# Four of seven Strassen-Winograd products added up in one PSUM bank, with their partial sums copied out by ScalarE

## The chip, the cores and the metric

The kernel runs on one core of a Trainium2 chip. In the profile the engines are PE (TensorE's matmuls) and PEld (its weight loads), DVE (VectorE), ACT (ScalarE), POOL (GpSimd) and SP (SyncE, which here only issues DMAs). The metric is device microseconds for one execution of the whole program; lower is better.

## The reference, cut to what matters

The program is one layer of a decoder trunk in float32, for 256 tokens of width 2048: a mixer with differential attention, a convolution and retention, then cross-attention, then a gated feed-forward net of hidden width 5632. What fills the time are its dense products:

```
proj = h @ w_in                      # 2048 x 14336
merged = sum over 3 branches of sigmoid(gates) * (y @ w_branch[i])
x = x + merged @ w_out
q = h @ wq ; k, v = split(m @ wkv) ; x = x + o @ wo
a, b = split(h @ w13) ; x = x + (silu(a) * b) @ w2
```

## The kernel before

**One product.** A float32 operand is split in two fp32r parts, hi (a rounded copy, made by an ACT cast into a tile `wh`) and lo (what is left, made by a DVE subtraction into `wl`). One 128 x 512 result then takes three matmuls for each 128 rows of weight: hi*hi, hi*lo and lo*hi (`products`). Weights come in chunks `raw` of 128 x 2 x 512 (512 KB) by DMAs from SP; there are ten `raw` buffers and five each of `wh` and `wl`. A **unit** is one chunk with its matmuls: 12 where it serves both halves of the tokens ("N"), 6 where it serves one ("S"). `emit_unit` makes the parts of up to four units ahead of the one that is multiplied, so the casts run until they wait for PE to give back a `wh` buffer.

**A pair.** `pair` computes two neighbouring blocks of 512 output columns, W0 and W1, for all 256 tokens. The 2048 rows of weight are four chunks of 512. With `MODES2` two of them go through Strassen-Winograd: seven products p1 to p7 in place of eight, on sums of weight blocks (made by DVE and by accumulating DMAs from POOL) and sums of activation blocks (made by `factors`). The other two chunks are plain N units. `MODES1` has one S chunk and three N chunks. There are 26 pairs: five for the gates, four for keys and values, two for `w_out`, one for `w_o`, ten for the feed-forward columns (numbers 1 to 10 here) and four for `w_2`. Between some of them lie plain blocks (`block`), and small side tasks (transposes, softmax, normalisation) are mixed in.

**PSUM.** Eight banks of 512 columns: two tiles `mm` of two banks (one column block for both token halves) and four tiles `tp` of one bank, shared with the side tasks. In a pair, `ps0` and `ps1` are `mm` tiles, `pp` holds `tp` tiles. p2 and p4 go to `ps0` and p3 to `ps1`, with the N units. p1, p5, p6 and p7 each get a `tp` bank (summed over the S chunks) and are combined outside PSUM: `join1` copies p1 to SBUF on ACT, `join5`, `join6` and `join7` are five DVE operations of 512 columns, and `done` adds what they left to `ps0` and to `ps1` with one DVE operation of 1024 columns each, before the block's `evac`.

**Order.** The tile framework places the instructions of each engine when the program is built and adds the semaphore waits. Engines run their own lists in order. A wait on a PSUM tile counts for the whole tile: a matmul into one bank of an `mm` tile waits for a copy out of the other bank too.

Of the kernel before, what the change touches and what calls it, by code (L numbers as in the profile page):

```python
# [13 lines left out]
ALU = mybir.AluOpType  # L14
# [43 lines left out]
def trunk(ctx, tc, xT, xtok, memT, memtok, w_in, w_br, w_out, w_q, w_kv, w_o, w_13, w_2,  # L58
          prm, cst, decay, gfin, out):
    nc = tc.nc  # L60
    P = 128
# [231 lines left out]
    def products(u, only=None, final=True):  # L293
        a = u["act"]
        for k in range(2):
            for ps, key, k0, t, kind in u["prods"]:
                if only is not None and t not in only:
                    continue
                ah, al = lhs(a, kind, (t, k0) if kind == "n" else t, k)
                o = ps[key]  # L300
                fl = (id(ps), key)
                pe.matmul(o, ah, u["hi"][:, k, :], start=fl in u["start"] and k == 0, stop=False)
                pe.matmul(o, ah, u["lo"][:, k, :], start=False, stop=False)
                pe.matmul(o, al, u["hi"][:, k, :], start=False, stop=fl in u["stop"] and k == 1)

    def emit_unit(i):
        while state["made"] < min(i + 1 + min(LA, 1 + i), len(units)):
# [24 lines left out]
    def quad_jobs(pp, ps0, ps1, w0, w1, a):  # L332
# [49 lines left out]
        def f3(u):  # L382
            r = raw(ix["b22"])
            add(t["a"], r)
            parts(u, r)
            raws.pop(ix["b22"])
# [18 lines left out]
    def pair(W0, W1, acts, modes, evac0, evac1):  # L405


        ps0, ps1, pp = {}, {}, {}
        xs = []
        us = []  # L410
        sset = [c for c in range(len(acts)) if modes[c] == "S"]
        nset = [c for c in range(len(acts)) if modes[c] == "N"]

        def enter():
            settle(3)
            cap[0] = 3
            pin[0] = True

        def join1():
            x0, x1 = S4([P, 2, 512]), S4([P, 2, 512])  # L420
            xs.extend([x0, x1])
            sc.copy(x0[:, 0, :], pp.pop(1))

        def join5():
            ve.tensor_tensor(out=xs[1][:, 1, :], in0=pp.pop(5), in1=xs[0][:, 0, :], op=ALU.add)

        def join6():

            p = pp.pop(6)
            ve.tensor_tensor(out=xs[1][:, 0, :], in0=p, in1=xs[1][:, 1, :], op=ALU.subtract)  # L430
            ve.tensor_tensor(out=xs[0][:, 1, :], in0=p, in1=xs[0][:, 0, :], op=ALU.subtract)

        def join7():
            p = pp.pop(7)
            ve.tensor_tensor(out=xs[0][:, 1, :], in0=p, in1=xs[0][:, 1, :], op=ALU.subtract)
            ve.tensor_tensor(out=xs[1][:, 1, :], in0=xs[1][:, 0, :], in1=p, op=ALU.subtract)
            cap[0] = 4

        def done(n, ps, evac):
            def f():  # L440
                x = xs[n]
                ve.tensor_tensor(out=x, in0=ps["m"], in1=x, op=ALU.add)
                xs[n] = None
                insb[0] = True
                evac(x)
                insb[0] = False
# [6 lines left out]
        def units_of(*names):  # L453
            return [q[n] for m in names for q in quads for n in m]

        first = units_of(("p1",), ("p2", "p5"), ("p3", "p6"))
        marks = {len(quads) - 1: join1, 3 * len(quads) - 1: join5, 5 * len(quads) - 1: join6}

        def marked(i, f):
            def g():  # L460
                u = f()
                if i in marks:
                    call(marks[i])
                return u
            return g

        us += mixed([marked(i, f) for i, f in enumerate(first)], n0)
        us += [f() for f in units_of(("p7",))]
        call(join7)
        us += mixed(units_of(("p4",)), n1[:len(n1) // 2])  # L470
        call(done(0, ps0, evac0))
        us += [f() for f in n1[len(n1) // 2:]]
        call(done(1, ps1, evac1))

        def unpin():
            pin[0] = False

        call(unpin)
        close(us)

    def pair_n(W0, W1, acts, evac0, evac1, after):
# [114 lines left out]
    def factors(a, q):  # L596
# [4 lines left out]
        for o, x, y, op in ((0, a22, a21, ALU.subtract), (2, a11, a21, ALU.subtract),  # L601
                            (1, a22, fv[:, 2], ALU.add), (3, a12, fv[:, 1], ALU.subtract)):
# [977 lines left out]
```

## Time and profile before

| | |
|---|---|
| three runs | 2001.64, 2002.55, 1997.3 us; median 2001.64 |
| the profiled execution | 1998.88 us, span 1997.1 us |
| PE, PEld | 1979.9 us (99%), 1636.8 us (82%), 9081 of each |
| DVE | 1666.9 us (83%) |
| ACT | 1120.4 us (56%) |
| TensorE's granted clock | 0.999 of full speed |

The pairs lie between about 500 and 1905 us of the span. Matmuls overlap in the profile: the record of one runs on while the next has started, so a busy PE is judged by the distance from one start to the next and by the idle time listed ahead of an instruction.

### The profile page before, as it was taken

The numbers are of one execution on the slowest core, as the hardware profiler recorded it, in microseconds if no ns is written. First come the engines' busy times: TensorE is split into PE (matmuls) and PEld (weight loads), VectorE is DVE, ScalarE is ACT, GpSimd is POOL, SyncE is SP. The second block draws the span as 40 slices with busy tenths as digits, with TensorE's granted clock in tenths as the row PEclk, the third lists the DMA queues.
The fourth block names the chain that finished last, engine by engine and source line by source line (L and its number), as shares of the span: only waits on it lengthen the run. The fifth ranks groups of instructions, "written<-read, shape, count | busy, mean of one in ns | idle before, by whom it ended". The sixth has DMA issues, their size and how long they took to land.

```text
span 1997.1 us, 25285 instructions
## 1 busy us (share of the span) xinstructions
PE 1979.9 (99%) x9081; PEld 1636.8 (82%) x9081; DVE 1666.9 (83%) x2040; ACT 1120.4 (56%) x1343; POOL 129.8 (6%) x172
## 2 busy tenths in 40 slices
PE   9999999999999999999999999999999999999998
PEld 7888888888788887888888888888888878878886
DVE  6997689778887788989988565899988999889974
ACT  7444343548655556655566554665655665655653
POOL 0000000000100001000111000000001000011000
PEclk9999999999999999999999999999999999999999
DMA  9656555554777788689898544957888978988891
GB/s 377 206 193 197 180 177 166 180 170 151 214 208 240 235 262 257 221 263 283 274 295 304 191 158 136 287 177 224 271 274 276 275 231 252 301 278 260 256 329 61
DMA packets 128285, 463.88 MB, mean 232 GB/s; under 512 B 14368, under 2 KB 14624, under 8 KB 128160
## 3 DMA queue, kind: packets, MB, share of 16 engines
q1 hardware_dynamic: 105552, 380.46, 54.1%
q0 software_dynamic: 22464, 81.80, 19.3%
q8 instruction: 71, 1.16, 0.2%
q14 instruction: 54, 0.44, 0.1%
q10 hardware_dynamic: 144, 0.01, 0.0%
HBM read 449.63 MB, written 12.58 MB: 231 GB/s over the span
## 4 chain that ended last, share of the span: by engine, by line
PE 79%; issue 9%; DVE 6%; DMA 4%; POOL 1%; ACT 1%; SPq 0%; ACTq 0%; POOLq 0%; DVEq 0%
PE mm L86 64%; PE tp L86 15%; DVE wl L86 3%; DVE s L86 2%; DMA raw<-in_w 2%; DMA raw<-in_w_kv 1%; DMA raw<-in_w_in 1%; POOL raw L94 1%; DVE raw L86 1%; ACT wh L86 1%; DMA s<-in_memtok 0%; SPq L97 0%; POOL s L94 0%; ACTq L1575 0%; POOL x2d L94 0%
## 5 line engine op out<-in xcount | busy, mean ns | idle before, releaser
L86 PE MATMUL mm<-wh,s 128*128 128x512 f32 x4568 | 1443.9, 391 | 3.5 <-ACT wh L86 3.3
L86 ACT CAST wh<-raw 128x1024 fp32r<-128x1024 f32 (+1 forms) x855 | 886.4, 1051 | 728.7 <-PE mm L86 474.9
L86 DVE TENSOR_TENSOR wl<-raw,wh 128x1024 fp32r<-128x1024 f32 (+1 forms) x855 | 1020.8, 1217 | 252.7 <-ACT wh L86 241.3
L86 PEld LDWEIGHTS mm<-wh,s 128*128 128x128 f32 x4568 | 857.7, 188 | 183.1 <-ACT wh L86 7.0
L86 PE MATMUL mm<-wl,s 128*128 128x512 f32 x2284 | 893.2, 391 | 4.4 <-DVE wl L86 4.4
L86 PEld LDWEIGHTS mm<-wl,s 128*128 128x128 f32 x2284 | 429.5, 188 | 97.3 <-DVE wl L86 9.3
L86 PE MATMUL tp<-wh,s 128*128 128x512 f32 x864 | 288.5, 392 | 0.0
L86 PEld LDWEIGHTS tp<-wh,s 128*128 128x128 f32 x864 | 162.2, 188 | 33.1
L86 PE MATMUL tp<-wl,s 128*128 128x512 f32 x432 | 168.1, 389 | 0.0
L86 DVE TENSOR_TENSOR s<-s,s 128x1024 f32<-128x1024 f32 (+4 forms) x144 | 140.8, 986 | 1.7 <-ACT wh L86 1.1
L86 DVE TENSOR_TENSOR s<-tp,s 128x512 f32<-128x512 f32 (+1 forms) x166 | 109.6, 683 | 16.4 <-PE tp L86 11.7
L86 DVE TENSOR_TENSOR raw<-raw,raw 128x1024 f32<-128x1024 f32 x100 | 121.0, 1216 | 0.4
L86 DVE SCALAR_TENSOR_TENSOR s<-s,prm_t,s 128x256 fp32r<-128x256 f32 (+25 forms) x256 | 105.8, 461 | 0.0
L86 DVE TENSOR_TENSOR s<-mm,s 128x1024 f32<-128x1024 f32 (+1 forms) x70 | 83.1, 1187 | 20.3 <-PE mm L86 20.1
L86 PEld LDWEIGHTS tp<-wl,s 128*128 128x128 f32 x432 | 81.2, 188 | 16.2
L86 ACT ACTIVATE s<-s 128x512 f32<-128x512 f32 (+1 forms) x60 | 46.2, 771 | 63.3 <-DVE s L86 51.4
L94 POOL DMA_DIRECT2D raw<-in_w x54 | 47.7, 883 | 431.8 <-DVE wl L86 188.4
L86 PE MATMUL tp<-cst_t,s 128*128 128x128 f32 x408 | 57.1, 272 | 0.0
L86 PEld LDWEIGHTS tp<-cst_t,s 128*128 128x128 f32 x408 | 48.6, 140 | 9.0 <-issue 0.3
L86 PE MATMUL tp<-s,s 128*128 128x256 f32 (+4 forms) x348 | 53.5, 314 | 0.0
L86 PEld LDWEIGHTS tp<-s,s 128*128 128x128 f32 (+1 forms) x348 | 46.1, 189 | 5.8 <-issue 0.5
L86 ACT COPY s<-tp 128x512 f32<-128x512 f32 (+1 forms) x69 | 35.8, 528 | 15.0 <-PE tp L86 13.3
(88 smaller groups left out, 503.2 us busy)
## 6 DMA issues: line engine op xcount, KB each, us to landing
raw<-in_w SPq DMA_DIRECT2D x264, 512.0 KB, 6.5
raw<-in_w_in SPq DMA_DIRECT2D x239, 512.0 KB, 4.6
raw<-in_w_kv SPq DMA_DIRECT2D x64, 512.0 KB, 5.4
raw<-in_w POOLq DMA_DIRECT2D x54, 512.0 KB, 8.5
raw<-in_w_br SPq DMA_DIRECT2D x48, 512.0 KB, 6.5
raw<-in_w_out SPq DMA_DIRECT2D x32, 512.0 KB, 7.6
raw<-in_w_q SPq DMA_DIRECT2D x32, 512.0 KB, 5.1
raw<-in_w_o SPq DMA_DIRECT2D x32, 512.0 KB, 4.0
```

The costliest lines, as they stand in the source:

```text
L86: i = f(*a, **k)
L94: tc.keep_in_program_order(nc.gpsimd.dma_start(**kw))
```

## The change

The roles of the two blocks change, and four products are added up by TensorE. p1, p6, p7 and p4 now go, in this order, to one bank of `ps1` (key 1), p2 to its other bank (key 0), and p3 to `ps0`; only p5 still has a `tp` bank, which it holds until after p7. ACT copies the state of the shared bank to SBUF after p1 (`keep1`), after p6 and after p7 (`keep`), and its end in `done1`. DVE subtracts the copies from p5 (`keep`, 512 columns twice), adds `ps0` (1024 columns) and one bank of `ps1` (512 columns). p6 moves ahead of p3 and takes the load of the block b22 with it; the last N unit of `ps0` moves behind p7, and `done0` with its `evac` ahead of p4. `factors` has other signs and as many operations.

```
-        return dict(p1=unit(pp, 1, 0, 0, "n", f1, b11=w0[:, 0:2, :]),
-                    p2=unit(ps0, 0, 2, 0, "n", f2, b21=b21, b12=w1[:, 0:2, :]), p5=unit(pp, 5, 0, 0, "s", f5),
-                    p3=unit(ps1, 0, 0, 3, "s", f3, b22=b22), p6=unit(pp, 6, 0, 1, "s", f6),
-                    p7=unit(pp, 7, 0, 2, "s", f7), p4=unit(ps0, 1, 2, 1, "n", f4))
+        return dict(p1=unit(c1, 1, 0, 0, "n", f1, b11=w0[:, 0:2, :]),
+                    p2=unit(c1, 0, 2, 0, "n", f2, b21=b21, b12=w1[:, 0:2, :]), p5=unit(pp, 5, 0, 0, "s", f5),
+                    p6=unit(c1, 1, 0, 1, "s", f6, b22=b22), p3=unit(c2, 0, 0, 3, "s", f3),
+                    p7=unit(c1, 1, 0, 2, "s", f7), p4=unit(c1, 1, 2, 1, "n", f4))
...
+        def keep1():
+            xs.extend([S4([P, 2, 512]), S4([P, 2, 512])])
+            sc.copy(xs[1][:, 0, :], ps1[1])
+
+        def keep(i):
+
             def f():
+                x = xs[0][:, i, :]
+                sc.copy(x, ps1[1])
+                ve.tensor_tensor(out=x, in0=pp[5], in1=x, op=ALU.subtract)
+                if i:
+                    pp.pop(5)
+                    cap[0] = 4
             return f
 
+        def done0():
+            x = xs[0]
+            ve.tensor_tensor(out=x, in0=ps0["m"], in1=x, op=ALU.add)
...
+        def done1():
+            x = xs[1]
+            ve.tensor_tensor(out=x[:, 0, :], in0=ps1[0], in1=x[:, 0, :], op=ALU.add)
+            sc.copy(x[:, 1, :], ps1[1])
...
-        quads = [quad_jobs(pp, ps0, ps1, W0[c], W1[c], acts[c]) for c in sset]
+        quads = [quad_jobs(pp, ps1, ps0, W1[c], W0[c], acts[c]) for c in sset]
...
+        us += mixed(units_of(("p1",), then=keep1) + units_of(("p2", "p5"))
+                    + units_of(("p6",), then=keep(0)) + units_of(("p3",)), n0[:-1])
+        us += [f() for f in units_of(("p7",), then=keep(1))]
+        us.append(n0[-1]())
+        call(done0)
         us += mixed(units_of(("p4",)), n1[:len(n1) // 2])
```

**First place: p7 and p4 in feed-forward pair 2, on PE.** Before, `tp_2335` is p7's bank, `mm_2297` is `ps0` and `mm_2319` is `ps1`; wh_2326 is p7's second unit, wh_2328 is p4's first:

```order
L86 MATMUL tp_2335_11878<-wh_2326_11834,s4_2190_11208 128x512
L86 MATMUL mm_2297_11695<-wh_2328_11844,s4_2163_11075 128x512
L86 MATMUL tp_2335_11878<-wl_2327_11835,s4_2190_11208 128x512
L86 MATMUL tp_2335_11878<-wh_2326_11834,s4_2191_11209 128x512
L86 MATMUL tp_2335_11878<-wh_2326_11834,s4_2190_11208 128x512
L86 MATMUL tp_2335_11878<-wl_2327_11835,s4_2190_11208 128x512
L86 MATMUL tp_2335_11878<-wh_2326_11834,s4_2191_11209 128x512
L86 MATMUL mm_2319_11798<-wh_2331_11858,s4_2207_11294 128x512
```

Now `mm_2245` is `ps1`, wh_2282 is p7's second unit and wh_2287 is p4's first, all in one bank:

```order
L86 MATMUL mm_2245_11615<-wl_2283_11777,s4_2154_11172 128x512
L86 MATMUL mm_2245_11615<-wh_2282_11776,s4_2155_11173 128x512
L86 MATMUL mm_2245_11615<-wh_2282_11776,s4_2154_11172 128x512
L86 MATMUL mm_2245_11615<-wl_2283_11777,s4_2154_11172 128x512
L86 MATMUL mm_2245_11615<-wh_2282_11776,s4_2155_11173 128x512
L86 MATMUL mm_2245_11615<-wh_2287_11798,s4_2127_11039 128x512
L86 MATMUL mm_2245_11615<-wl_2288_11799,s4_2127_11039 128x512
L86 MATMUL mm_2245_11615<-wh_2287_11798,s4_2128_11040 128x512
```

p4 began in a bank of its own while p7 still ran; now it follows p7 in the same bank with nothing between, and its first matmul waits for the copy that ACT makes of that bank after p7's last. So it stands in pairs 1, 2, 5 and 6 of the feed-forward net; in the first pair of the gates two 128 x 128 transposes lie between; in the other 21 pairs there are 11 to 13 matmuls there.

**Second place: from feed-forward pair 9 to pair 10, on ACT.** Before, the end of the pair has no operation on ACT; `s4_3088` is pair 9's first result, and the casts wh_3145 on are of its last units and of the next pair's first:

```order
L86 ACTIVATE s4_3088_15441<-s4_3088_15441 128x1024
L86 CAST wh_3145_15711<-raw_3143_15705 128x1024
L86 CAST wh_3148_15729<-raw_3147_15727 128x1024
L86 CAST wh_3150_15747<-raw_3137_15673 128x1024
L86 CAST wh_3158_15771<-raw_3156_15765 128x1024
L86 CAST wh_3163_15788<-raw_3162_15786 128x1024
L86 CAST wh_3167_15804<-raw_3140_15685 128x1024
L86 CAST wh_3170_15825<-raw_3169_15822 128x1024
```

Now `mm_3008` is pair 9's `ps1`, and the copy is that of `done1`:

```order
L86 CAST wh_3072_15651<-raw_3062_15599 128x1024
L86 CAST wh_3075_15672<-raw_3074_15670 128x1024
L86 CAST wh_3083_15696<-raw_3081_15690 128x1024
L86 COPY s4_3017_15370<-mm_3008_15337 128x512
L86 CAST wh_3087_15711<-raw_3065_15611 128x1024
L86 CAST wh_3091_15729<-raw_3062_15599 128x1024
L86 CAST s4_3078_15683<-tp_3080_15685 128x512
```

One copy has been put between the casts of the next pair's units. The cast ahead of it (wh_3083) waits until PE has given back the `wh` of pair 10's p1; the copy waits for `done1`'s addition on DVE as well. PE's list has p1 of pair 10 (12 matmuls, in the tile that `ps0` left), and then the first N unit into the tile that this copy empties: from the matmul that frees wh_3083's buffer to that N unit there are six matmuls. It is so at ten ends of a pair: that of the first `w_out` pair and nine among the feed-forward and `w_2` pairs; at the others there are more matmuls or a plain block.

**Third place: p6 and p7 in feed-forward pair 1 (`MODES1`), on ACT.** Before, there are casts alone between the parts of p6, p7 and p4; s4_2239 is a part of an activation factor, made by `factors`:

```order
L86 CAST wh_2247_11458<-raw_2193_11215 128x1024
L86 CAST wh_2251_11473<-raw_2250_11471 128x1024
L86 CAST wh_2254_11491<-raw_2253_11489 128x1024
L86 CAST wh_2257_11509<-raw_2256_11507 128x1024
L86 CAST s4_2239_11425<-s4_2235_11401 128x1024
L86 CAST wh_2261_11524<-raw_2260_11522 128x1024
L86 CAST wh_2264_11536<-raw_2263_11534 128x1024
L86 CAST wh_2267_11554<-raw_2266_11552 128x1024
```

Now `mm_2175` is `ps1`, and the last row stands for the copies after p6 and after p7:

```order
L86 CAST wh_2210_11422<-raw_2157_11179 128x1024
L86 CAST wh_2213_11434<-raw_2212_11432 128x1024
L86 CAST wh_2216_11452<-raw_2215_11450 128x1024
L86 CAST wh_2219_11466<-raw_2218_11464 128x1024
L86 CAST s4_2203_11388<-s4_2199_11365 128x1024
L86 COPY s4_2180_11285<-mm_2175_11268 128x512 x2
```

The copy after p6 has moved behind wh_2219 and s4_2203. wh_2219 waits for the last matmul ahead of p7 on PE (its `wh` buffer), and p7's first matmul waits for the copy; p4 then follows p7 directly and waits for the second copy.

## Rows read from the trace of the kernel before

**Rows 1.** Page, part 1: engine, busy us (share of span) xinstructions.
```profile
span 1997.1 us, 25285 instructions
PE 1979.9 (99%) x9081; PEld 1636.8 (82%) x9081; DVE 1666.9 (83%) x2040; ACT 1120.4 (56%) x1343; POOL 129.8 (6%) x172
```

**Rows 2.** Busy time of each engine by stretch.
```profile
core 0: us, PE busy (x) PEld busy (x) DVE busy (x) ACT busy (x) POOL busy (x), PEclk, DMA share, GB/s
500.00:1905.00 1405.00, 1397.54 (x6380) 1157.80 (x6379) 1204.87 (x1248) 819.55 (x934) 120.65 (x158) 1.00 0.80 246
...
700.00:1100.00 400.00, 397.74 (x1785) 327.75 (x1784) 355.81 (x372) 241.12 (x288) 40.00 (x55) 1.00 0.86 271
...
1300.00:1900.00 600.00, 596.00 (x2662) 491.86 (x2661) 547.53 (x540) 354.79 (x366) 54.86 (x69) 1.00 0.84 256
...
```

**Rows 3.** Waits of the span: engine and line, releaser, us, times, longest.
```profile
PEld mm L86 <- DVE wl L86: 9.3, 13, 1.4
...
PEld mm L86 <- ACT wh L86: 7.0, 8, 1.6
...
PE mm L86 <- DVE wl L86: 4.4, 7, 1.0
...
PE mm L86 <- ACT wh L86: 3.3, 5, 1.2
```

**Rows 4.** Timeline 1545.6 to 1549.6 us: start, us, engine, line, operation [idle before <-releaser].
```profile
1546.13 0.61 PE L86 MATMUL tp<-wh,s 128*128 128x512 f32 x2
...
1546.82 0.61 PE L86 MATMUL tp<-wh,s 128*128 128x512 f32 x2
...
1547.49 0.39 PE L86 MATMUL tp<-wh,s 128*128 128x512 f32 x1
...
1547.72 0.39 PE L86 MATMUL mm<-wh,s 128*128 128x512 f32 x1
...
1547.92 0.59 ACT L86 COPY s<-tp 128x512 f32<-128x512 f32 x1 [0.26 <-PE tp L86]
...
1548.40 2.00 ACT L86 CAST wh<-raw 128x1024 fp32r<-128x1024 f32 x2
```

**Rows 5.** Timeline 1700 to 1702 us.
```profile
1700.45 0.39 PE L86 MATMUL mm<-wh,s 128*128 128x512 f32 x1
1700.62 1.99 ACT L86 CAST wh<-raw 128x1024 fp32r<-128x1024 f32 x2 [5.23 <-DMA raw<-in_w]
...
1701.72 0.50 PE L86 MATMUL mm<-wh,s 128*128 128x512 f32 x1 [0.88 <-ACT wh L86]
```

**Rows 6.** Groups of ACT, shapes apart: count | busy us, mean ns | idle before.
```profile
L86 ACT CAST wh<-raw 128x1024 fp32r<-128x1024 f32 x853 | 885.2, 1052 | 727.2 <-PE mm L86 474.9 <-DMA raw<-in_w 63.0 <-PE tp L86 39.5
...
L86 ACT COPY s<-tp 128x512 f32<-128x512 f32 x50 | 28.8, 589 | 6.0 <-PE tp L86 4.3 <-DVE s L86 1.7
L86 ACT CAST s<-s 128x1024 fp32r<-128x1024 f32 x24 | 25.2, 1049 | 10.1 <-DVE s L86 10.0
```

**Rows 7.** Groups of DVE, shapes apart, same columns.
```profile
L86 DVE TENSOR_TENSOR wl<-raw,wh 128x1024 fp32r<-128x1024 f32 x853 | 1019.4, 1218 | 251.1 <-ACT wh L86 239.7 <-DMA raw<-in_w_in 5.1 <-DMA raw<-in_w_q 4.5
...
L86 DVE TENSOR_TENSOR s<-mm,s 128x1024 f32<-128x1024 f32 x66 | 80.3, 1217 | 5.2 <-PE mm L86 5.0
L86 DVE TENSOR_TENSOR s<-tp,s 128x512 f32<-128x512 f32 x108 | 71.7, 683 | 11.8 <-PE tp L86 11.7
...
L86 DVE TENSOR_TENSOR s<-s,tp 128x512 f32<-128x512 f32 x26 | 17.6, 676 | 0.0
```

**Rows 8.** Timeline of ACT near 1375 us, and at 1575 us.
```profile
1375.51 1.06 ACT L86 CAST wh<-raw 128x1024 fp32r<-128x1024 f32 x1 [1.89 <-PE mm L86]
...
1575.18 3.90 ACT L86 CAST wh<-raw 128x1024 fp32r<-128x1024 f32 x4
```

More of the change, by code (lines that the diff above doesn't have):

```diff
@@ L301, in products @@
                 fl = (id(ps), key)
-                pe.matmul(o, ah, u["hi"][:, k, :], start=fl in u["start"] and k == 0, stop=False)
-                pe.matmul(o, ah, u["lo"][:, k, :], start=False, stop=False)
-                pe.matmul(o, al, u["hi"][:, k, :], start=False, stop=fl in u["stop"] and k == 1)
+                sk = dict(skip_group_check=True) if ps.get("open") and key == 1 else {}
+                pe.matmul(o, ah, u["hi"][:, k, :], start=fl in u["start"] and k == 0, stop=False, **sk)
+                pe.matmul(o, ah, u["lo"][:, k, :], start=False, stop=False, **sk)
+                pe.matmul(o, al, u["hi"][:, k, :], start=False, stop=(fl in u["stop"] or "ends" in u) and k == 1, **sk)
     def emit_unit(i):
@@ L330, in block, with quad_jobs @@
         call(lambda: evac(ps["m"]))
-    def quad_jobs(pp, ps0, ps1, w0, w1, a):
+    def quad_jobs(pp, c1, c2, w0, w1, a):
         def unit(ps, key, k0, t, kind, fn, **w):
@@ L380, in f5, with f3 @@
             parts(u, t["a"])
[L382 to L386, printed above, removed]
         def f6(u):
+            t["r"] = raw(ix["b22"])
+            add(t["a"], t["r"])
             parts(u, t["a"])
             gd(out=t["a"], in_=b21, accum_op=ALU.add)
+        def f3(u):
+            parts(u, t.pop("r"))
+            raws.pop(ix["b22"])
         def f7(u):
@@ L396, in f4 @@
             parts(u, t.pop("a"))
-        return dict(p1=unit(pp, 1, 0, 0, "n", f1, b11=w0[:, 0:2, :]),
-                    p2=unit(ps0, 0, 2, 0, "n", f2, b21=b21, b12=w1[:, 0:2, :]), p5=unit(pp, 5, 0, 0, "s", f5),
-                    p3=unit(ps1, 0, 0, 3, "s", f3, b22=b22), p6=unit(pp, 6, 0, 1, "s", f6),
-                    p7=unit(pp, 7, 0, 2, "s", f7), p4=unit(ps0, 1, 2, 1, "n", f4))
+        return dict(p1=unit(c1, 1, 0, 0, "n", f1, b11=w0[:, 0:2, :]),
+                    p2=unit(c1, 0, 2, 0, "n", f2, b21=b21, b12=w1[:, 0:2, :]), p5=unit(pp, 5, 0, 0, "s", f5),
+                    p6=unit(c1, 1, 0, 1, "s", f6, b22=b22), p3=unit(c2, 0, 0, 3, "s", f3),
+                    p7=unit(c1, 1, 0, 2, "s", f7), p4=unit(c1, 1, 2, 1, "n", f4))
     insb = [False]
     def pair(W0, W1, acts, modes, evac0, evac1):
-        ps0, ps1, pp = {}, {}, {}
+        ps0, ps1, pp = {}, {"open": True}, {}
         xs = []
@@ L416, in enter @@
             cap[0] = 3
[L417 to L439, printed above, removed]
-            def f():
[L441 to L446, printed above, removed]
-            return f
+        def keep1():
+            xs.extend([S4([P, 2, 512]), S4([P, 2, 512])])
+            sc.copy(xs[1][:, 0, :], ps1[1])
@@ new lines, in keep @@
+        def keep(i):
+            def f():
+                x = xs[0][:, i, :]
[4 more added lines that the diff above has]
+                    cap[0] = 4
+            return f
+        def done0():
+            x = xs[0]
+            ve.tensor_tensor(out=x, in0=ps0["m"], in1=x, op=ALU.add)
+            xs[0] = None
+            insb[0] = True
+            evac0(x)
+            insb[0] = False
@@ L449, in pair @@
+        def done1():
+            x = xs[1]
+            ve.tensor_tensor(out=x[:, 0, :], in0=ps1[0], in1=x[:, 0, :], op=ALU.add)
+            sc.copy(x[:, 1, :], ps1[1])
+            xs[1] = None
+            insb[0] = True
+            evac1(x)
+            insb[0] = False
         call(enter)
-        quads = [quad_jobs(pp, ps0, ps1, W0[c], W1[c], acts[c]) for c in sset]
+        quads = [quad_jobs(pp, ps1, ps0, W1[c], W0[c], acts[c]) for c in sset]
         n0, n1 = (each_half(ps, [W[c] for c in nset], [acts[c] for c in nset]) for ps, W in ((ps0, W0), (ps1, W1)))
-        def units_of(*names):
-            return [q[n] for m in names for q in quads for n in m]
@@ L456, in pair, with units_of, last @@
[L456 to L463, printed above, removed]
-                return u
[L465 to L469, printed above, removed]
+        def units_of(*names, then=None):
+            fs = [q[n] for m in names for q in quads for n in m]
+            def last():
+                u = fs[-1]()
+                u["ends"] = True
+                call(then)
+                return u
+            return fs if then is None else fs[:-1] + [last]
@@ L470, in pair @@
+        us += mixed(units_of(("p1",), then=keep1) + units_of(("p2", "p5"))
[3 more added lines that the diff above has]
+        call(done0)
         us += mixed(units_of(("p4",)), n1[:len(n1) // 2])
-        call(done(0, ps0, evac0))
         us += [f() for f in n1[len(n1) // 2:]]
-        call(done(1, ps1, evac1))
-        def unpin():
-            pin[0] = False
@@ L478, in pair @@
-        call(unpin)
+        call(done1)
         close(us)
@@ L600, in factors @@
         a11, a12, a21, a22 = (q[:, 2 * k:2 * k + 2, t * P:(t + 1) * P] for t in range(2) for k in range(2))
-        for o, x, y, op in ((0, a22, a21, ALU.subtract), (2, a11, a21, ALU.subtract),
-                            (1, a22, fv[:, 2], ALU.add), (3, a12, fv[:, 1], ALU.subtract)):
+        for o, x, y, op in ((0, a21, a22, ALU.subtract), (2, a11, a21, ALU.subtract),
+                            (1, fv[:, 0], a11, ALU.subtract), (3, a12, fv[:, 1], ALU.add)):
             ve.tensor_tensor(out=fv[:, o], in0=x, in1=y, op=op)
```

## The prediction

> **What bounds the kernel now.** I read the page's table of engines first, then the busy time by stretch, the waits, and a few microseconds of timeline. PE is busy for 1979.9 of the span's 1997.1 us [rows 1]. A busy PE may still run slower than it could, so I looked at starts: with 128x512 matmuls following each other, the one at 1546.13 and the one at 1547.49 are six apart, 1.36/6 = 0.227 us each, and where nothing is listed as idle it keeps that step [rows 4]. What is left for any other engine to spoil is small: between 500 and 1905 us, where all 26 pairs lie, PE is idle for 1405.00 - 1397.54 = 7.5 us [rows 2]. The waits that PE names there are for `wl` and `wh`, 4.4 and 3.3 us in the whole span, and for its weight loads 9.3 and 7.0 us, which overlap [rows 3]. One such place is at 1701.72: a cast waited 5.23 us for its weights, and PE lost 0.88 us [rows 5]. So PE is the bound, DVE is close behind (355.8 of 400 us from 700, 547.5 of 600 us from 1300), and ACT has room (354.8 of 600) [rows 2]. The casts spend 474.9 us waiting for PE to hand back a buffer [rows 6]: the stages behind PE run ahead of it as far as their buffers let them.
>
> **What the change removes.** The number of matmuls, their shapes and their weight loads stay as they are, and so does the step of 0.227 us: PE's own work is worth 0. DVE loses three operations in each pair. Before: four of 0.683 and one of 0.676 us (the latter group has 26 members, one for each pair) and two of 1.217; after: three of 0.683 and one of 1.217 [rows 7]. That is 5.84 - 3.27 = 2.57 us a pair, 26 x 2.57 = 67 us of DVE. In the stretch from 1300, which holds 14 of the pairs, DVE falls from 547.5 by 36 to about 512 of 600 us. None of it stands on PE's path except where PE waited for a late `wl`. The bounds of this gain are 0 and the whole 7.5 us; part of those 7.5 is late weights, as at 1701.72, which a freer DVE helps only through buffers that come back sooner. I take 3 us.
>
> **What it adds on ACT.** One PSUM copy a pair becomes four. The one of before took 589 ns [rows 6], so it is 3 x 0.589 x 26 = 46 us; from 1300 on, ACT rises by 14 x 1.77 = 25 to 380 of 600 us. As sheer work that is hidden behind PE. What counts is that PE now waits for these copies: after p6 and after p7 the next product goes to the bank that ACT is reading.
>
> The price of one such wait comes from the copy of p1 in the kernel before. The last p1 matmul starts at 1547.49, and its record ends 0.39 later, at 1547.88; the copy starts at 1547.92 and ends at 1548.51 [rows 4]. PE starts 0.05 us after ACT has ended: the cast of 1700.62 takes 1.05, and PE goes on at 1701.72 [rows 5, 6]. From the last matmul's start to the next into the same bank that is 0.39 + 0.04 + 0.59 + 0.05 = 1.07 us, where PE alone would take 0.23: **0.84 us** if nothing stands between. With eleven matmuls between, 12 x 0.227 = 2.72 us have gone by, and the wait is covered with 1.65 us to spare, even behind one more cast of 1.05.
>
> Place by place, from the order of the changed kernel:
> - p7 to p4 back to back, in feed-forward pairs 1, 2, 5 and 6: 4 x 0.84 = 3.4 us. In the first gate pair two small transposes stand between; I count 0.6. The other 21 pairs have 11 to 13 matmuls there and count 0, covered by the last N unit.
> - p6 to p7 in feed-forward pair 1. PE's last matmul frees a buffer; ACT casts wh_2219 (0.95 us to the next start in a row of casts, (3.90 - 1.05)/3 [rows 8]), casts an activation factor (0.95; 1.049 alone [rows 6]), and then copies: 0.39 + 0.04 + 0.95 + 0.95 + 0.59 + 0.05 - 0.23 = 2.7 us.
> - The ten ends of a pair where ACT has cast, copy, and PE six matmuls until it wants the tile: 0.39 + 0.04 + 0.95 + 0.59 + 0.05 = 2.02 against 7 x 0.227 = 1.59: 0.43 us each, 4.3 together. That the cast ahead of the copy does wait for PE, so that no slack is left in it, is what the 1.89 us at 1375.51 show of its kind [rows 8]; if it runs early, this item is 0.
> - p1 to p2: p2 lies in the same tile and waits for the copy of p1. There are at least six matmuls between in every pair (1.36 us more than the step, against 0.84), and three places where short ACT operations stand ahead of the copy: 0 to 1 us each. I take 1 us in all.
>
> The sum is 3.4 + 0.6 + 2.7 + 4.3 + 1 = 12.0 us.
>
> **What moves.** b22's load on SP and its addition come with p6 instead of p3, one or two units earlier, and its `raw` buffer of ten is held until p3's parts are made: SP's later loads may come a unit later, and the casts waited for weights for 63.0 us even before [rows 6]. Against that, DVE returns buffers sooner. POOL's second accumulating DMA, issued after that addition, comes earlier too, and p4 wants it later. I take 0 for these, between -2 and +6 us: a late weight has cost 0.88 us once [rows 5], and six more of it would be 6. p5's bank is held longer, but p1, p6 and p7 give theirs back to the side tasks. The signs in `factors` cost nothing: as many operations in as long a chain. `done0` comes earlier, which takes its 1.217 us out of the crowd around p4 [rows 7].
>
> **The sum.** -3 + 12.0 + 0 = +9 us on the profiled execution's 1998.88: 2007.9. That execution lies 2.8 us below the median of the three runs, 2001.64, so a median could come out up to 2.8 higher; I forecast **2009 us**. With the items at their ends the forecast's own range is 2005 to 2016.
>
> **The rivals.**
>
> *No change to be told (31%).* A stall of PE gives SP, ACT and DVE time to catch up. The new waits could then take the place of the 7.5 us that PE was idle anyway, and the ten ends of pairs could cost nothing if their casts run early: 3.4 + 0.6 + 2.7 + 1 - 5 = +3 us, 2002 to 2005 as above. For it speaks that the old idle time lies in the same stretches; against it, that the back-to-back places stand in the order whatever else happens.
>
> *Faster (5%).* If all of the 7.5 us goes back to DVE's lag, and the copies start while PE is held up by something else, the kernel ends at 1998.9 - 7.5 = 1991. The point from which it decides is 0: the new waits have to be below what DVE gives back. A stronger form is that DVE sets the pace wherever it is 89 to 91% busy, so that its 67 us come off whole: 1998.9 - 67 = 1932. The trace speaks against it: matmuls follow each other at a steady 0.227 us with DVE at that share, and PE's idle time bounds the gain at 7.5 us [rows 2, 4]; I give it 1 of the 5%. The Trainium skill (Perfetto Trace Analysis, Identifying the Most-Contended Engine) would lean to that form: it ranks engines by occupancy, but has TensorE judged by the occupancy of its weight loads since matmul records overlap, and PEld's 82% lies below DVE's share. Here the trace disagrees, as the even step of the matmuls shows.
>
> *Much slower (12%).* The copy after p7 blocks ACT's list. In 21 pairs it is covered by 11 to 13 matmuls, 1.65 us to spare, but if the cast ahead of it waits for weights, as casts did 22 times for one source alone [rows 6], the copy is late as well and PE stops with work at hand. At 0.84 us for each of 21 pairs it adds 18 us: 2007.9 + 18 = 2026. It decides from about 1.65 us of lateness. Against it: with the same weights late, PE would often have had to wait in the kernel before.
>
> **How the numbers follow.** Forecast 52%, no change 31%, much slower 12%, faster 5%. A measurement of this kernel can tell about 0.3% from no change, 6 us; nearly all of the forecast's case lies past that, and I count it as slower. So slower 0.64, same 0.31, faster 0.05. The range from 1999 to 2022 takes in the forecast's own, most of the case of no change and a half of the much slower one.
>
> **What would show it.** In the changed profile DVE's total falls by some 67 us and ACT's rises by 46; the copies out of `mm` are 104, near 0.59 us each. PE's idle time from 500 to 1905 us rises from 7.5 to about 16, and waits of PE on an ACT copy appear: 0.84 us at p4 in feed-forward pairs 1, 2, 5, 6, one of about 2.7 us in pair 1, and about 0.4 us at ends of pairs. Wrong would be: no wait of PE behind a copy; PE's idle time below 7.5 us; a step of matmuls other than 0.227 us; or new idle time that names `wl` or late weights instead.

## The result

The changed kernel takes 2016.87 us (median of six runs, 2014.67 to 2022.03) where the kernel before takes 2000.73 (six runs): a ratio of 1.0085, 95% interval 1.0070 to 1.0101, which is 14 to 20 us. The forecast was slower by 7 to 9 us; it is slower by 16. The profiled execution is the slowest of the six, 2022.03 us; what follows explains that one first and then what is usual.

Page, part 1, of the changed kernel:

```profile
span 2020.3 us, 25231 instructions
PE 1990.8 (99%) x9081; PEld 1640.3 (81%) x9081; DVE 1624.5 (80%) x1962; ACT 1161.7 (58%) x1421; POOL 129.8 (6%) x172
```

The same 9081 matmuls [rows 1]; DVE is busy for 42 us less, ACT for 41 us more, and the program is longer. Busy time by stretch, all the pairs first, then three short stretches (columns as in [rows 2]):

```profile
500.00:1905.00 1405.00, 1388.05 (x6287) 1145.22 (x6286) 1146.86 (x1156) 845.88 (x996) 114.89 (x150) 0.99 0.79 243
793.00:800.00 7.00, 6.72 (x19) 5.48 (x20) 6.45 (x9) 5.31 (x7) 2.87 (x5) 0.54 0.70 242
1374.00:1380.00 6.00, 5.50 (x14) 4.40 (x15) 4.27 (x4) 3.40 (x4) 0.00 (x0) 0.53 0.32 104
1805.00:1811.00 6.00, 5.84 (x19) 4.67 (x20) 6.00 (x7) 3.05 (x4) 0.00 (x0) 0.72 0.95 358
```

PE is idle for 17.0 us (1405.00 - 1388.05) where it was 7.5 [rows 2]. Look also at the third column from the end: in the three short stretches the mean granted clock is 0.54, 0.53 and 0.72 of full speed, between the levels of 1.2 and 2.4 GHz (0.50 and 1.00) and in two of them close to the lower. In the kernel before it was 1.00 in every stretch shown [rows 2]. What PE waits for (columns as in [rows 3]):

```profile
PEld mm L86 <- ACT s L86: 23.6, 23, 3.2
...
PE mm L86 <- ACT s L86: 13.8, 19, 2.7
...
PEld mm L86 <- DVE wl L86: 5.3, 8, 1.4
...
PE mm L86 <- DVE wl L86: 2.7, 5, 1.1
PE mm L86 <- ACT wh L86: 2.0, 4, 1.2
```

The old waits for `wl` and `wh` shrank from 4.4 and 3.3 us to 2.7 and 2.0 [rows 3]; the 13.8 us behind ACT's `s`, which are its copies of the shared bank, are new. The copies themselves, and the DVE operations that answer to [rows 6, 7]:

```profile
L86 ACT COPY s<-mm 128x512 f32<-128x512 f32 x104 | 60.5, 586 | 20.4 <-PE mm L86 19.9 <-DVE s L86 0.3
L86 DVE TENSOR_TENSOR s<-mm,s 128x1024 f32<-128x1024 f32 x40 | 48.7, 1219 | 2.9 <-PE mm L86 2.8
L86 DVE TENSOR_TENSOR s<-tp,s 128x512 f32<-128x512 f32 x56 | 38.3, 685 | 5.9 <-PE tp L86 4.2 <-ACT s L86 1.6
...
L86 DVE TENSOR_TENSOR s<-mm,s 128x512 f32<-128x512 f32 x30 | 20.6, 686 | 18.0 <-PE mm L86 18.0
```

**The three predicted waits** are where they were put. Feed-forward pair 2, p7's last matmul, the copy, p4's first (timeline of PE and ACT):

```profile
1423.20 0.39 PE L86 MATMUL mm<-wh,s 128*128 128x512 f32 x1
1423.63 0.59 ACT L86 COPY s<-mm 128x512 f32<-128x512 f32 x1 [0.30 <-PE mm L86]
...
1424.27 0.50 PE L86 MATMUL mm<-wh,s 128*128 128x512 f32 x1 [0.68 <-ACT s L86]
...
1424.61 0.39 PE L86 MATMUL mm<-wl,s 128*128 128x512 f32 x1
```

From start to start 1.07 us, so 0.84 lost, the price that the prediction made from [rows 4, 5]. (The bracket shows less, 0.68, since the record of the last matmul runs on.) The last row shows a part of the price that nobody had: behind the wait one more step takes 0.34 us (1424.61 - 1424.27) and not 0.227. It is so behind nearly every wait of both kernels, 0.11 us each time, and makes the whole price of such a wait 0.95. The end of pair 2 has the cast, the copy behind it, and the matmul that wants the tile:

```profile
1439.61 1.05 ACT L86 CAST wh<-raw 128x1024 fp32r<-128x1024 f32 x1 [0.30 <-PE mm L86]
...
1440.50 0.39 PE L86 MATMUL mm<-wh,s 128*128 128x512 f32 x1
1440.57 0.57 ACT L86 COPY s<-mm 128x512 f32<-128x512 f32 x1
...
1441.19 0.50 PE L86 MATMUL mm<-wh,s 128*128 128x512 f32 x1 [0.31 <-ACT s L86]
```

0.69 from start to start where 0.23 is the step: 0.46 lost, for a predicted 0.43; the same wait stands at nine ends in the feed-forward net (`w_2` taken in). At a tenth, near 1050 us, the copy waits for DVE's addition as well, and 0.65 us are lost. And p6 to p7 in feed-forward pair 1, with the copy behind a cast and a part of an activation factor, then the copy after p7:

```profile
1368.80 0.39 PE L86 MATMUL mm<-wh,s 128*128 128x512 f32 x1
1369.22 1.04 ACT L86 CAST wh<-raw 128x1024 fp32r<-128x1024 f32 x1 [1.66 <-PE mm L86]
1370.17 1.04 ACT L86 CAST s<-s 128x1024 fp32r<-128x1024 f32 x1
1371.12 0.58 ACT L86 COPY s<-mm 128x512 f32<-128x512 f32 x1
1371.75 0.50 PE L86 MATMUL mm<-wh,s 128*128 128x512 f32 x1 [2.56 <-ACT s L86]
...
1374.50 0.80 PE L86 MATMUL mm<-wh,s 128*128 128x512 f32 x1 [0.68 <-ACT s L86]
...
1375.52 1.06 PE L86 MATMUL mm<-wh,s 128*128 128x512 f32 x2
...
1376.80 1.06 PE L86 MATMUL mm<-wh,s 128*128 128x512 f32 x2
```

2.72 us lost, as predicted (1371.75 - 1368.80, less one step). But look at the last two rows: three matmuls in 1.28 us, a step of 0.427 and not 0.227. This is the low clock of the stretch above; it sets in behind the wait.

**Two waits that no term of the sum had.** In the last pair of the gates the copy after p6 stands behind a square for the statistics of `mem`, which waits for its own load; in a pair of `w_2` the copy after p7 stands behind a cast whose weights are late (each fence shows the operation that waits, the copy, and the matmul that wants the bank):

```profile
791.42 0.63 ACT L86 ACTIVATE s<-s 128x512 f32<-128x512 f32 x1 [4.09 <-DMA s<-in_memtok]
...
792.66 0.56 ACT L86 COPY s<-mm 128x512 f32<-128x512 f32 x1
...
793.28 0.80 PE L86 MATMUL mm<-wh,s 128*128 128x512 f32 x1 [2.74 <-ACT s L86]
```

```profile
1803.57 1.04 ACT L86 CAST wh<-raw 128x1024 fp32r<-128x1024 f32 x1 [1.83 <-DMA raw<-in_w]
1804.52 0.58 ACT L86 COPY s<-mm 128x512 f32<-128x512 f32 x1
...
1805.15 0.50 PE L86 MATMUL mm<-wh,s 128*128 128x512 f32 x1 [2.12 <-ACT s L86]
```

Both have 11 or more matmuls between the product and the next one into the bank. That would have covered a copy that is on time, and did not cover these; by the starts PE lost 2.9 and 2.3 us. The low clock comes with each of the two as well.

### The profile page after: what moved, and what is told of

The parts are those of the page before. It is cut to its first block, busy times and chain, and to the rows that moved or that the text cites. A ratio compares the mean times of both kernels' runs of the same rounds, so it can differ in the third digit from the quotient of the medians.

```text
span 2020.3 us, 25231 instructions
## 1 busy us (share of the span) xinstructions
PE 1990.8 (99%) x9081; PEld 1640.3 (81%) x9081; DVE 1624.5 (80%) x1962; ACT 1161.7 (58%) x1421; POOL 129.8 (6%) x172
## 4 chain that ended last, share of the span: by engine, by line
PE 90%; DVE 3%; DMA 2%; issue 2%; ACT 2%; POOL 0%; SPq 0%; ACTq 0%; POOLq 0%; DVEq 0%
PE mm L86 81%; PE tp L86 9%; DVE s L86 1%; DVE wl L86 1%; ACT wh L86 1%; DMA raw<-in_w 1%; ACT s L86 1%; DMA raw<-in_w_out 1%; DMA s<-in_memtok 1%; DMA raw<-in_w_in 0%; DVE raw L86 0%; SPq L97 0%; POOL raw L94 0%; ACT L86 0%; ACTq L1572 0%
## 5 line engine op out<-in xcount | busy, mean ns | idle before, releaser
L86 PE MATMUL mm<-wh,s 128*128 128x512 f32 x5168 | 1627.5, 392 | 17.0 <-ACT s L86 13.8
L86 PEld LDWEIGHTS mm<-wh,s 128*128 128x128 f32 x5168 | 972.8, 188 | 229.4 <-ACT s L86 23.6
L86 PE MATMUL mm<-wl,s 128*128 128x512 f32 x2584 | 1011.5, 392 | 2.7 <-DVE wl L86 2.7
L86 PEld LDWEIGHTS mm<-wl,s 128*128 128x128 f32 x2584 | 487.0, 188 | 104.5 <-DVE wl L86 5.3
L86 PE MATMUL tp<-wh,s 128*128 128x512 f32 x264 | 88.7, 394 | 0.0
L86 DVE TENSOR_TENSOR s<-tp,s 128x512 fp32r<-128x512 f32 (+1 forms) x114 | 76.0, 684 | 10.5 <-ACT s L86 5.9
L86 ACT COPY s<-mm 128x512 f32<-128x512 f32 x104 | 60.5, 586 | 20.4 <-PE mm L86 19.9
L86 PEld LDWEIGHTS tp<-wh,s 128*128 128x128 f32 x264 | 49.6, 188 | 10.0
L86 PE MATMUL tp<-wl,s 128*128 128x512 f32 x132 | 51.4, 390 | 0.0
L86 ACT CAST s<-tp 128x512 fp32r<-128x512 f32 x58 | 31.5, 587 | 10.1 <-PE tp L86 10.0
```

Of the source, the lines that this page charges most:

```text
L86: i = f(*a, **k)
```

## The experiments

Theory A: the loss is PE waiting behind ACT's copies, and what follows from these waits. Theory B: the moved order (p6 and b22 ahead of p3, the last N unit behind p7) costs by itself. Theory C: the low clock comes by itself. Theory D, added before e9: p1's place in the second block's tile wants both tiles at once at a pair's start, and that costs whichever engine empties the tile. Times of each group are compared with runs of the kernel before beside them: 2002.83 us for e1 to e4, 2001.13 for e5 to e8, 2000.20 for e9 to e12. The ratio goes by all runs and is not the quotient of two medians.

| | us | ratio to before, 95% |
|---|---|---|
| changed kernel | 2016.87 | 1.0085 (1.0070 to 1.0101) |
| e1 no copies after p6, p7 | 2007.67 | 1.0028 (1.0018 to 1.0039) |
| e2 end added on DVE | 2013.88 | 1.0058 (1.0045 to 1.0072) |
| e3 PE and ACT pinned, all pairs | 2042.96 | 1.0208 (1.0193 to 1.0224) |
| e4 e3 and e2 | 2046.85 | 1.0225 (1.0210 to 1.0241) |
| e5 ACT pinned, feed-forward | 2018.11 | 1.0078 (1.0065 to 1.0092) |
| e6 both kinds of pair | 2010.99 | 1.0046 (1.0033 to 1.0059) |
| e7 before, p6 ahead of p3 | 1997.50 | 0.9979 (0.9970 to 0.9989) |
| e8 more copies | 2059.42 | 1.0283 (1.0265 to 1.0301) |
| e9 no copies but p1's | 2000.85 | 1.0002 (0.9993 to 1.0010) |
| e10 before, N unit behind p7 | 2001.41 | 1.0002 (0.9994 to 1.0011) |
| e11 p1, p2, p5 first | 2036.34 | 1.0176 (1.0162 to 1.0190) |
| e12 N unit between p7 and p4 | 2015.53 | 1.0075 (1.0060 to 1.0089) |

**e1 and e9: the copies left out.**

```
e1:              x = xs[0][:, i, :]
-                sc.copy(x, ps1[1])
-                ve.tensor_tensor(out=x, in0=pp[5], in1=x, op=ALU.subtract)
+                ve.tensor_tensor(out=x, in0=pp[5], in1=xs[1][:, 0, :], op=ALU.subtract)
e9, as well:
-            sc.copy(x[:, 1, :], ps1[1])
```

DVE subtracts the copy of p1 in place of the copies left out, and in e9 POOL fills the half tile that the last copy would have filled; neither kernel computes the reference's second block.

> The changed kernel without the ACT copies after p6 and after p7 (52 of the 104; DVE subtracts an SBUF tile from p5's bank instead, so what is computed there is not the product sums). The matmuls, the loads and the place of b22 stay. Theory A, PE's waits for these copies, with late copies behind other ACT work and the lower granted clock that follows the longest of them: the four waits of 0.84, the one of 2.7, those at 793 us (2.7) and 1805 us (2.1) and the low clock behind them go, 12 to 17 us; 2000 to 2005 us, PE idle near 10 us from 500 to 1905. Theory B, the moved order itself (b22 earlier, the last N unit behind p7, done0 earlier, POOL's second accumulating DMA): all of that is still here, so at most 3 us go; 2014 to 2017. Theory C, the low clock comes by itself and not behind the waits: only the 10 to 11 us of waits go, and stretches at half clock stay in the profile.

> The changed kernel with only the copy of p1's state left: those after p6 and p7 and the one at a pair's end are left out (the second block is then not the reference's). The order, the loads and the place of the four products stay. Theory A, every loss is a wait behind an ACT copy of the shared bank or what follows from it: the 0.47 us at nine pair ends go as well as what the first run took away, 4 to 6 us less than the first run's 2007.7, so 2001 to 2004 and, beside the kernel with the new order alone (1997.5), 4 to 6 us for late casts near 790 to 850 us. Theory D, the place of p1 in the second block's tile wants both tiles at once at a pair's start, and that costs whoever empties the tile: the waits stay at pair ends, now behind DVE, and the time stays near 2007.

Without the copies after p6 and p7 the ratio falls by 0.57 points, 11 us; without the one at the end of a pair by another 0.26, 5 us, and the time is that of the kernel before. So most of the loss hangs on the copies, and theory B, which expected e1 near 2015, falls. In detail e1 missed: 2007.7 for 2000 to 2005, since the pair ends are still in it (they are A's too, and my expectation left them out). e9 lies at the lower edge of its range (2000.85 for 2001 to 2004), and theory D falls for the pair ends: with DVE emptying the tile they are free. PE in e9 over all pairs:

```profile
500.00:1905.00 1405.00, 1398.57 (x6385) 1159.44 (x6384) 1163.42 (x1175) 826.06 (x937) 134.88 (x183) 1.00 0.80 247
```

6.4 us of idle time for 7.5 before [rows 2], at a mean clock of 1.00. But half of it is one wait of the kind that theory D had in mind, near 836 us, and the clock falls with it (the last row is a stretch of 5 us, columns as in [rows 2]):

```profile
835.05 1.21 DVE L86 TENSOR_TENSOR s<-mm,s 128x1024 f32<-128x1024 f32 x1
...
836.41 0.47 PE L86 MATMUL mm<-wh,s 128*128 128x512 f32 x1 [3.27 <-DVE s L86]
```

```profile
836.00:841.00 5.00, 4.59 (x13) 3.71 (x14) 5.00 (x7) 1.05 (x1) 0.00 (x0) 0.66 0.81 221
```

The same wait stands in e1 (3.19 us) and, shorter, in the changed kernel (1.01), and not in the kernel before. So what e1 and e9 win may understate what the copies cost, by up to about 4 us in these profiles (3.3 for the wait and 1.6 for the clock, less 1.0).

**e7 and e10: the order alone, in the kernel before.**

```
e7:  -  p3=unit(ps1, 0, 0, 3, "s", f3, b22=b22), p6=unit(pp, 6, 0, 1, "s", f6),
     +  p6=unit(pp, 6, 0, 1, "s", f6, b22=b22), p3=unit(ps1, 0, 0, 3, "s", f3),
     -  first = units_of(("p1",), ("p2", "p5"), ("p3", "p6"))
     +  first = units_of(("p1",), ("p2", "p5"), ("p6",), ("p3",))
e7 and e10:
     -  us += mixed([marked(i, f) for i, f in enumerate(first)], n0)
     +  us += mixed([marked(i, f) for i, f in enumerate(first)], n0[:-1])
        us += [f() for f in units_of(("p7",))]
     +  us.append(n0[-1]())
```

> The kernel before with only the order of the change: p6 with b22's load and sum ahead of p3, and the last N unit of the first block behind p7. All four products keep their own banks, the DVE operations stay. Theory A: no wait behind a copy is added, so within 2 us of the kernel before. Theory B: the moved loads and sums cost by themselves what the changed kernel loses before 1345 us, 5 to 10 us, 2006 to 2012.

> The kernel before with one piece of the order alone: the last N unit of the first block behind p7. p6 stays behind p3, and b22 comes with p3. If the gain of the seventh run (0.2%, 3.6 us) comes from this unit, which puts 12 matmuls between p7 and p4 and gives the parts of p4 more time: 1996 to 1999. If it comes from b22's earlier load and sum: 2000 to 2002, level with the kernel before.

Both theories missed e7: the order is worth 4 us (0.11 to 0.30%) in the other direction, and e7 is the fastest kernel of this study, faster than both that were given. e10 puts the gain on p6 and b22 and not on the N unit. Where it comes from shows in how long casts waited for the weights of the feed-forward net. e7, and then e10:

```profile
ACT wh L86 <- DMA raw<-in_w: 16.2, 8, 4.4
```

```profile
ACT wh L86 <- DMA raw<-in_w: 56.5, 28, 6.2
```

63.0 us before [rows 6], 16.2 with b22 loaded ahead. Late weights, like those at 1701 us [rows 5], are fewer when p6 and b22 come earlier. That it is the load and not p6's place in the order is argued from these rows; no run moves one without the other. Why SP gets ahead by it I did not follow further.

**e2, e3, e4, e5, e6: covering the waits instead.** e2 gives the pair's end back to DVE, e3 pins PE and ACT to the program's order from p6 to p4 in all pairs, e4 does both; e5 pins ACT alone in the feed-forward net, e6 has that with the old pairs in the earlier stages.

```
e2:  +  nc.gpsimd.memset(xs[1][:, 1, :], 0.0)
     -  ve.tensor_tensor(out=x[:, 0, :], in0=ps1[0], in1=x[:, 0, :], op=ALU.add)
     -  sc.copy(x[:, 1, :], ps1[1])
     +  ve.tensor_tensor(out=x, in0=ps1["m"], in1=x, op=ALU.add)
e3:  -PIN = ()
     +PIN = ("pe", "act")     # pin[0] is set at p6's first unit, cleared after p4's stretch
e5:  +PIN = ("act",)          # pin[0] is set at the feed-forward net's start, cleared at its end
```

> The changed kernel with the copy at a pair's end taken from ACT: POOL clears that half of the SBUF tile early, and DVE adds the whole of ps1 in one operation of 1024 columns, as in the kernel before; 26 ACT copies less, DVE 26 x 0.53 us more. Theory A: the ten waits of 0.43 to 0.47 us at pair ends go or shrink to about 0.1 us, 3.5 to 4.7 us; 2012 to 2013.5 us. Theory B: nothing of it changes; 2015 to 2018.

> The changed kernel with PE and ACT kept in the order in which the program is written, from p6 to the end of p4's stretch of each pair. An N unit then lies between p7 and p4 in all 26 pairs (12 matmuls), and ACT's copy after p6 stands ahead of the casts that wait for later matmuls. All copies stay. Theory A: the waits at p4 (4 x 0.84) and at p7 in feed-forward pair 1 (2.7, and the low clock behind it, 2 to 4) go, those at 793 and 1805 us may stay; 7 to 10 us less, 2006 to 2010. Theory B: the loads and b22 come as early as in the changed kernel; 2014 to 2018. Against both: a fixed order makes PE wait for late weights that it could have gone round, then 2017 or more, with waits for wh and wl.

> The last two edits together. Theory A: both gains add up, 11 to 15 us less than the changed kernel, 2001.5 to 2006; whether DVE's relief (now about 28 us of busy time less than before) is worth anything shows here: below the kernel before by 2 to 3 us, or level with it. Theory B: 2013 to 2018.

> The changed kernel with ACT alone kept in the order in which the program is written, and only in the feed-forward net (its pairs and those of w_2, from about 1345 us on); the side tasks of the earlier stages, at which the pinned order of the third run lost 26 us, are left alone. All copies stay; in the order the copies after p6 and p7 have at least 2.49 us of matmuls behind them in these 14 pairs, and the copy at a pair's end 4 us or more. Theory A (PE's waits behind ACT copies): from 1345 us on nothing of the 12.9 us that the changed kernel loses there in its profile is left, and 3 to 5 us come back since DVE is freer; in all 13 to 18 us less than the changed kernel, 1999 to 2004. Theory B (moved loads and sums of weights, which this kernel has too): at most 5 us less, 2012 to 2017.

> Pairs as in the kernel before up to cross-attention (12 of them), pairs of the changed kernel in the feed-forward net (14), there with ACT in the program's order. Theory A: no wait behind an ACT copy is left, and in the 14 pairs DVE has three operations less: 2 to 6 us below the kernel before, 1995 to 2000; if the freer DVE is worth nothing, level with it. Theory B (the moved order costs by itself): half of 16 us, about 8 above the kernel before.

e2's time is near what was expected, for another reason: the wait at a pair's end is still there, and has only changed its name, since DVE's 1.22 us of addition now stand ahead of the `wl` that PE wants next (pair 2's end in e2):

```profile
1433.31 0.50 PE L86 MATMUL mm<-wl,s 128*128 128x512 f32 x1 [0.31 <-DVE wl L86]
```

What e2 gains lies near 793 and 1805 us, where its copies are not late, and near 1366, where the same wait ahead of p7 is not followed by the low clock. e3 and e4 lose some 25 and 28 us more than the changed kernel: a pinned PE stops at small side tasks that the framework's order had gone round. These waits, for DVE's `s` ahead of matmuls into `tp`, are 25.6 us at seven places in e3 and 0.5 us in the changed kernel. One of them in e3:

```profile
543.50 0.48 PE L86 MATMUL tp<-cst_t,s 128*128 128x128 f32 x1 [8.54 <-DVE s L86]
```

From the feed-forward net on, e3 loses only 2 us on the kernel before (by the starts of equal matmuls, 41.4 us behind at its 1390, 43.3 at the end), where the changed kernel loses 12.9. In e5 and e6 most copies come in time, and yet little or nothing is won: in e5 five waits behind a copy are left in the feed-forward net (0.28 to 1.07 us idle), and casts come late where the copies had been, so that PE stops once or twice a pair, as here in e5:

```profile
1393.04 0.50 PE L86 MATMUL mm<-wh,s 128*128 128x512 f32 x1 [0.44 <-ACT wh L86]
```

```profile
1408.60 0.50 PE L86 MATMUL mm<-wl,s 128*128 128x512 f32 x1 [0.51 <-DVE wl L86]
```

Theory A's numbers for e3 to e6 were all wrong: they took a wait that is covered for a wait that is gone. Theory B's number for e6, 8 us above the kernel before, came out (9), but not for its reason, since the order alone costs nothing (e7).

**e11 and e12: other orders.**

```
e11: -  us += mixed(units_of(("p1",), then=keep1) + units_of(("p2", "p5"))
     -              + units_of(("p6",), then=keep(0)) + units_of(("p3",)), n0[:-1])
     +  us += [f() for f in units_of(("p1",), then=keep1) + units_of(("p2", "p5"))]
     +  us += mixed(units_of(("p6",), then=keep(0)) + units_of(("p3",)), n0[:-1])
e12: PE pinned from p7 to the end of p4's stretch, in the feed-forward net alone
```

> The changed kernel with the units of p1, p2 and p5 ahead of all N units of a pair, and the N units mixed with p6 and p3 instead. All copies stay; in the order at least 2.49 us of matmuls lie behind every copy after p6 and p7, but for the first gate pair of two S chunks on (0.22 once, in the keys and values). Theory A: the waits at p4 (4 x 0.84), at p7 in feed-forward pair 1 (2.7) and the low clock behind it go, 6 to 9 us; 2008 to 2011. But at the pair ends of the feed-forward net transposes of the finished block now stand six matmuls behind the cast ahead of the copy and wait for the copy and for a DVE product of 1.22 us as well: (0.39 + 0.04 + 0.95 + 0.59 + 1.22 + 0.05) - 1.59 = 1.65 us each, at up to seven ends; with these 2016 to 2022.

> The changed kernel with PE kept in the program's order from p7 to p4 in the 14 pairs of the feed-forward net and of w_2, so that the last N unit (12 matmuls) lies between them in feed-forward pairs 1, 2, 5 and 6 too; nothing else is ordered, and the copy after p6 in pair 1 stays where it is. By the prediction's price 4 x 0.84 = 3.4 us less than the changed kernel: 2013 to 2014.5, and the wait of 2.7 us at p7 stays. Theory B or C: 2016 to 2018.

In e11 the waits at p7 and p4 are gone from the feed-forward net, and the pair ends cost far more, 2.43 us by the starts at nine of them: transposes of the finished block wait for the copy and for the product behind it.

```profile
1442.53 1.05 ACT L86 CAST wh<-raw 128x1024 fp32r<-128x1024 f32 x1 [0.30 <-PE mm L86]
...
1443.49 0.58 ACT L86 COPY s<-mm 128x512 f32<-128x512 f32 x1
...
1444.81 1.22 DVE L86 TENSOR_TENSOR s<-s,s 128x1024 f32<-128x1024 f32 x1
...
1446.08 0.44 PE L86 MATMUL tp<-cst_t,s 128*128 128x128 f32 x2 [2.27 <-DVE s L86]
```

The expectation saw the chain and left out that DVE is still busy with `wl` (the product starts 0.74 us after the copy's end), and the earlier stages, where five waits of 1.7 to 3.4 us stand (by the starts) and e11 is 9 us further behind than the changed kernel when the feed-forward net begins. e12 takes the four waits at p4 away; its time lies above the range expected, and its 1.0075 for 1.0085 neither shows the 3.4 us nor excludes them, as the intervals overlap; its wait at p7 in pair 1 has grown from 2.7 to 4.5 us by the starts.

**e8: the price, and the clock.** In the 14 late pairs the copy after p7 is made one to five times. The last N unit stands ahead of p7 again, so that nothing lies between p7 and p4; ACT is pinned as in e5, and PE from p7 to p4 in these 14 pairs.

```
-                sc.copy(x, ps1[1])
+                if i and pin[0]:
+                    doses.append(1 + len(doses) % 5)
+                for _ in range(doses[-1] if i and pin[0] else 1):
+                    sc.copy(x, ps1[1])
```

> The changed kernel with ACT in the program's order in the feed-forward net, and with nothing between p7 and p4 in any of the 26 pairs (the N unit ahead of p7 again); in the 14 late pairs ACT makes the copy after p7 one to five times over, in turn 1, 2, 3, 4, 5. By the prediction's price PE loses 0.84 us for one copy and 0.5 to 0.59 more for each further one, so 1.4, 1.9 to 2.0, 2.5 to 2.6 and 3.0 to 3.2: with 12 early pairs at 0.84 and 14 late ones 33 to 38 us above the kernel of the fifth run at an even clock. If the low granted clock follows long idle times, it is seen behind the doses of four and five and not behind one or two, and adds 2 to 4 us at each; if it comes by itself, it is seen anywhere or nowhere.

p4's first matmul behind one, two, three, four and five copies (timeline of PE, five places):

```profile
1380.31 0.50 PE L88 MATMUL mm<-wh,s 128*128 128x512 f32 x1 [0.68 <-ACT s L88]
...
1429.23 0.50 PE L88 MATMUL mm<-wh,s 128*128 128x512 f32 x1 [1.29 <-ACT s L88]
...
1473.48 0.50 PE L88 MATMUL mm<-wh,s 128*128 128x512 f32 x1 [1.91 <-ACT s L88]
...
1518.38 0.50 PE L88 MATMUL mm<-wh,s 128*128 128x512 f32 x1 [2.53 <-ACT s L88]
...
1791.57 0.50 PE L88 MATMUL mm<-wh,s 128*128 128x512 f32 x1 [3.15 <-ACT s L88]
```

The first copy costs 0.84 us by the starts, each further one 0.62, a little over the 0.50 to 0.59 expected. The whole kernel lies 41 us above e5, 33 to 38 were expected at an even clock; the step of 0.34 behind each wait was in no price. Two stretches behind four copies, the one at 1518 and the one at 1744 us:

```profile
1518.00:1525.00 7.00, 6.62 (x29) 5.51 (x30) 6.45 (x6) 4.24 (x5) 0.56 (x1) 1.00 0.60 212
...
1744.00:1751.00 7.00, 6.51 (x22) 5.23 (x23) 4.28 (x4) 3.88 (x5) 0.00 (x0) 0.76 0.31 111
```

The same wait, once with the clock at 1.00 and 29 matmuls in the stretch, once at 0.76 and 22. The expectation for doses of four and five came out in part: the low clock followed two of three places with four copies, one of two with five, and one of three with three.

## Why the prediction was right and wrong

**Right:** PE bounds the kernel, and its step is 0.227 us before and after. The operations that change on DVE lose 65 us by their groups (67 predicted); the page's total falls by only 42, since the 853 `wl` operations take 10 us more in all and records that overlap count once in it. ACT's rise was 41 for 46. The places of the three waits were right, and so were their sizes up to the next matmul's start: 0.84 at p7 to p4, 2.7, and 0.46 at nine ends and 0.65 at a tenth for a predicted 0.43 at ten. Between p1 and p2 two waits show, near 776 and 1263, 0.4 us each; 1 us was taken for all. The 0.6 of the first gate pair does not show: no wait of PE ahead of 776 us names a copy.

The rule of the Trainium skill that the prediction weighed (Perfetto Trace Analysis, Identifying the Most-Contended Engine) ranks by occupancy and, with TensorE taken by its weight loads (one of the two measures that it gives), would have had DVE relieved first, 83% against 82%. Here DVE was relieved, and the time did not fall.

PE's idle time came out as foreseen, 17.0 us for about 16, but by luck: 4.9 us of it are the two waits that no term had, and the waits for `wl` and `wh` over the pairs had shrunk from 7.3 to 1.8 us, by more than the 3 us taken.

**Wrong, first step: the term for the copies after p6 and p7.** 3.4 + 0.6 + 2.7 = 6.7 us were taken; leaving these copies out is worth 11 us (1.0085 to 1.0028). The working held that 11 matmuls between two products cover a copy, even behind one more cast, and counted such places as 0. Two copies were later than that, behind ACT operations that waited for DMAs, and cost 2.9 and 2.3 us by the starts. This is the mechanism of the rival that I named much slower, at 2 places and not at 21.

**Second step: the sum had no term for the clock.** With the three waits of over 2 us came 34 matmuls at a step of about 0.427 us, 34 x 0.2 = 7 us in the profiled execution. The six runs show how far this differs from one to the next: 2014.67 and 2014.69 us at a mean granted clock of 0.999, 2022.03 at 0.994. I estimate from these that at full clock the loss is about 14 us, and that the usual run adds some 2.

**Third step: the relief of DVE, -3, and the moved loads, 0.** Their sum was right by chance. With the order alone (e7) the kernel gains 4 us, outside the bounds of -2 to +6 that the moved loads had, and casts wait less for weights. In e9 DVE has three operations a pair less on top of that order, and the time is not lower than e7's but 3 to 5 us higher (1.0002 against 0.9979). So the gain that I gave to DVE is there without DVE's relief. What a freer DVE is worth by itself is not shown: e9 also has p1 in its new place, and no run changes DVE's load alone. Of the difference between e7 and e9 a part is the wait near 836 us: between 700 and 850 us e9 falls back 2.8 us on e7 by the starts of equal matmuls. The rest is open; their profiled executions differ by only 2.2 us in all.

**The ends of pairs,** 4.3 us taken, are worth 5 (e1 to e9). The whole by ratios, in us: order -4, place of p1 and the rest +5, ends +5, copies after p6 and p7 +11, together 17; the prediction's terms were -3, +1, +4.3 and +6.7. Each of these steps carries 2 to 4 us of uncertainty. The starts of matmuls in the profiled execution give the same account from another side. Between 500 and 1905 us it loses 16.9 us at waits behind copies, 7.0 in matmuls at the low step and 1.3 more than before in the steps of 0.34, and gains 7.2 at waits for `wl` and `wh`.

**The rivals.** No change and faster are excluded by the interval. In the form where DVE sets the pace, its 65 us would have come off; they did not, and PE's step stayed at 0.227 us.

## What to carry to other kernels

Putting partial sums in one accumulator turns copies that nobody waited for into links of the critical engine's chain: price each by the last matmul, the copy and the restart, and then ask what can stand ahead of the copy in its engine's list, waits for DMAs above all. A wait that the order covers isn't gone: forcing an order to cover it moved it to casts or side tasks here. Test the pieces of a change one at a time: the one thought neutral here, p6 with its load ahead of p3, was the only gain that can be seen.

## What was not expected of the hardware

The granted clock falls behind some waits of PE and not behind others of the same length. The wait of 2.73 us ahead of p7 in feed-forward pair 1 stands in the changed kernel and in e2. In the first the stretch from 1374 us reads 0.53 (above); in e2, where the wait ends at 1366.44, the clock stays at 1.00 and PE starts or ends 32 matmuls in 7 us:

```profile
1369.00:1376.00 7.00, 7.00 (x32) 5.76 (x32) 5.17 (x5) 3.77 (x5) 0.00 (x0) 1.00 0.40 137
```

In e11 one of the nine waits of 2.43 us was followed by the low clock and eight were not. Theory C is not borne out: from 500 us to each program's last stretch, all 24 stretches at the lower level in the fourteen profiles begin within a wait of PE or at most 1.5 us behind one. What decides between two waits of one length stays open. Where the clock fell in the changed kernel, 7 to 13 matmuls took about 0.43 us each, some 1.4 to 2.6 us in all, as much as the wait itself.
